# Partial sums reloaded into PSUM by ScalarE, head norms on VectorE, and maximum and exponential in one step, in a one-core hybrid mLSTM and attention block

## The chip, the cores and the metric

The kernel runs on one core of one Trainium2 chip. The metric is the device time of one execution, in microseconds; lower is better. Five engines run their own instruction queues in order: TensorE (PE), VectorE (DVE), ScalarE (ACT), GpSimd (POOL) and SyncE (SP), which here only issues DMAs.

## The reference

One transformer-like layer over 256 tokens of width 2048, all in float32:

```python
mod = jnp.einsum('bd,de->be', jax.nn.silu(c), w_ada[layer]) + b_ada[layer]
shift1, scale1, gate1, shift2, scale2, gate2 = jnp.split(mod[:, None, :], 6, axis=-1)
h = rms_norm(x, norm1_w[layer]) * (1 + scale1) + shift1
proj = h @ w_in[layer]
mq, mk, mv, mo, mi, mf, dq, dk, dv = jnp.split(proj, split_pts, axis=-1)
...
h_ml = mlstm_chunkwise(to_heads(mq, ML_DQK), to_heads(mk, ML_DQK), to_heads(mv, ML_DV), li, lf)
h_ml = rms_norm(jnp.transpose(h_ml, (0, 2, 1, 3)), mlstm_norm_w[layer])
...
dq = partial_rope(rms_norm(dq.reshape(B, S, DA_HEADS, 2, DA_DH), q_norm_w[layer]), positions)
dk = partial_rope(rms_norm(dk.reshape(B, S, DA_HEADS, 2, DA_DH), k_norm_w[layer]), positions)
o_da = diff_attention(dq, dk, dv, lam)
o_da = rms_norm(o_da, subln_w[layer]) * (1.0 - lambda_init)
mix = jnp.concatenate([h_ml, o_da], axis=-1) @ w_out[layer]
x = x + gate1 * mix
h = rms_norm(x, norm2_w[layer]) * (1 + scale2) + shift2
g, u = jnp.split(h @ w_gate_up[layer], 2, axis=-1)
x = x + gate2 * ((jax.nn.silu(g) * u) @ w_down[layer])
```

The six modulation vectors come from a matrix-vector product with 2048 x 12288 weights (w_ada). Attention has 8 heads with two softmax maps each; the mLSTM has 4 heads.

## The kernel before, in words

**Ticks.** All large products are cut into 392 ticks, called T0 to T391 below. One tick takes a half chunk of weights (128 x 1024), splits it into a high and a low part in float32r, and does 12 matmuls of 128x512: three products (high x high, low weight x high, high weight x low; lines 581 to 583) for two rows and two token blocks. Per tick ACT casts the high part `wh` (line 211, called at `weights_hi`), DVE subtracts for the low part `wl` (line 181, `weights_lo`), and SP loads the raw weights `r` (line 527; 3 buffers). `wh` and `wl` have 4 buffers each, so they can be made up to about three ticks ahead of the product that reads them.

**The order of the ticks.** T0 to T95 are the input projection, twelve column groups, in six sweeps over the 2048 rows (`SWEEPS`; row blocks p0 to p1 of 256 rows, where one tick is one block): T0-11 and T12-23 one block for each group, T24-43 two blocks for ten groups, T44-67 four blocks (4 to 8) for the six EARLY groups (attention q and k, mLSTM q and k), T68-79 six blocks (2 to 8) for the two attention v groups, T80-95 four blocks for the mLSTM v and output gates. T96-127 are the output projection (`wo`), T128-151, T152-187 and T188-223 three sweeps of the gate and up projection (`f0`, `f1`, `f2`), T224-303 its rest (`fr`), T304-391 the down projection (`dn`). The unit "one sweep over one group" is called a visit. A visit accumulates in one of two PSUM accumulators of 128x1024 (pool `psA`); when it ends, `project_done` puts the sum away in SBUF as `proj[g]`: the first visit of a group by an ACT copy, each later one by a DVE addition `proj + acc` (line 181).

**Small work between ticks.** Everything else is written as generators whose steps (separated by `yield`) the class `Plan` (lines 90 to 161) places between the half ticks: the modulation columns `modc` and the transposed, normalised activations `hh`/`hl` (`make_hT`), attention (`prep`, `attend`, `attend_values`, `finish_attention`), the mLSTM (`conv`, `ml_scores`, `ml_values`, `ml_norm`, `ml_out`) and the gate rows (`g1rd`, `g1rp`). `Plan` keeps an estimate `v` of how far DVE's queue is behind and `a` for ACT's; it issues no new step while either is above 2.3 us (VMAX, AMAX), and never two steps of one generator in one place. The steps use 4 further PSUM banks (`psM`). An engine that is not PE thus gets its instructions in the order in which `Plan` issues them, and PE's transposes and small matmuls stand between the ticks at places fixed at build time. What a tick needs (`ready`) is forced to be issued ahead of it by `plan.until`.

**Norms of the heads.** The reciprocal square roots of q, k (`prep`: `rsq`, `rsk` in scratch, results `sclq` and `rstk`), of the attention output (`finish_attention`: `of`) and of the mLSTM output (`ml_norm`: `mf`) start from an integer estimate on DVE (`rsqrt_first`, lines 190 and 192) and take three Newton steps of four instructions on POOL (`rsqrt_newton`, lines 401 to 404). The scaled maximum of a softmax map, `st`, is also a POOL multiplication (line 785).

**Modulation weights.** 192 tiles of 512 KB (`ada`, 4 buffers) come by DMA. 40 of them go to PE as matrix-vector products (`gv`, line 216), the others to DVE as a multiplication with an accumulated sum (line 185). `ADA_PLAN` and `due(i)` say how many must be used by which tick; `ada_idle` uses further ones where the estimated DVE queue is short. The last 32 (for gate2, `ada5`) are held back until the stage `fr`.

## Time and profile before

| | |
|---|---|
| runs, us | 1230.78, 1231.78, 1232.55; median 1231.78 |
| profiled execution | 1227.86 us, of it 1226.1 us from the first to the last instruction |
| mean granted TensorE clock | 0.992 |
| busy share of the span | PE 97%, DVE 69%, ACT 47%, POOL 4% |
| `wl` subtraction on DVE | 392 of 1221 ns |
| `wh` cast on ACT | 392 of 1058 ns |
| modulation tile on DVE | 152 of 1217 ns |

In a line of the timeline the first number is the start in us, the second the duration; the bracket gives the idle time of the engine ahead of the instruction, and the instruction that it waited for. Rows that follow each other without a bracket ran back to back; since DVE and ACT overlap the end of one instruction with the start of the next, the distance of two starts (1.14 us for two `wl`) is what an instruction costs there. For PE the distance of two 128x512 matmuls is 0.227 us at full clock, so that a tick takes 2.73 us.

### The profile page before, as it was taken

The numbers are of one execution on the slowest core, as the hardware profiler recorded it, in microseconds if no ns is written. First come the engines' busy times: TensorE is split into PE (matmuls) and PEld (weight loads), VectorE is DVE, ScalarE is ACT, GpSimd is POOL, SyncE is SP. The second block draws the span as 40 slices with busy tenths as digits, with TensorE's granted clock in tenths as the row PEclk, the third lists the DMA queues.
The fourth block names the chain that finished last, engine by engine and source line by source line (L and its number), as shares of the span: only waits on it lengthen the run. The fifth ranks groups of instructions, "written<-read, shape, count | busy, mean of one in ns | idle before, by whom it ended". The sixth has DMA issues, their size and how long they took to land.

```text
span 1226.1 us, 14849 instructions
## 1 busy us (share of the span) xinstructions
PE 1189.7 (97%) x5590; PEld 955.9 (78%) x5590; DVE 851.1 (69%) x1197; ACT 582.1 (47%) x791; POOL 50.4 (4%) x126
## 2 busy tenths in 40 slices
PE   6999899998999898999999999999999999999998
PEld 2767678777888686788888888888888878888886
DVE  3757968898888998879856667878555454545443
ACT  3754345565666345665444444444444443433342
POOL 1000001205022000000000000000000000000000
PEclk9999999999999999999999999999999999999999
DMA  9898987656578897899755547998655544646471
GB/s 343 320 363 321 376 324 251 252 207 234 183 257 314 315 355 279 307 337 344 276 186 184 188 169 291 353 351 319 233 178 196 189 172 172 225 169 238 157 257 52
DMA packets 63258, 313.81 MB, mean 256 GB/s; under 512 B 6993, under 2 KB 7377, under 8 KB 41169
## 3 DMA queue, kind: packets, MB, share of 16 engines
q1 hardware_dynamic: 63186, 312.86, 69.9%
q8 instruction: 44, 0.72, 0.2%
q14 instruction: 28, 0.23, 0.0%
HBM read 310.73 MB, written 2.10 MB: 255 GB/s over the span
## 4 chain that ended last, share of the span: by engine, by line
PE 77%; DVE 13%; issue 3%; DMA 2%; POOL 2%; ACT 2%; SPq 0%; DVEq 0%; POOLq 0%; ACTq 0%
DVE wl L181 5%; DVE ada L185 4%; DMA ada<-in_w_ada_dram 2%; PE acc('dn', 0)_7816 L583 2%; PE acc('dn', 0)_7816 L581 2%; PE acc('dn', 2)_8616 L583 2%; PE acc('dn', 2)_8616 L581 2%; PE acc('dn', 1)_8236 L583 2%; PE acc('dn', 1)_8236 L581 2%; PE acc('dn', 0)_7816 L582 2%; PE acc('dn', 2)_8616 L582 2%; PE acc('dn', 1)_8236 L582 2%; DVE proj L181 1%; PE gv L216 1%; PE at L220 1%
## 5 line engine op out<-in xcount | busy, mean ns | idle before, releaser
L181 DVE TENSOR_TENSOR wl<-r,wh 128x1024 fp32r<-128x1024 f32 x392 | 473.6, 1221 | 206.6 <-ACT wh L211 206.3
L211 ACT ACTIVATE wh<-r 128x1024 fp32r<-128x1024 f32 x392 | 410.5, 1058 | 391.3 <-DMA r<-in_w_gu_dram 42.1
L185 DVE SCALAR_TENSOR_TENSOR ada<-ada,silc 128x1024 f32<-128x1024 f32 x152 | 183.0, 1217 | 1.7 <-DMA ada<-in_w_ada_dram 1.7
L216 PE MATMUL gv<-ada,early 128*32 128x256 f32 x320 | 25.7, 424 | 11.9 <-DMA ada<-in_w_ada_dram 11.7
L581 PE MATMUL acc('dn', 0)_7816<-wh,aTh 128*128 128x512 f32 x88 | 35.9, 408 | 0.0
L583 PE MATMUL acc('dn', 0)_7816<-wh,aTl 128*128 128x512 f32 x88 | 34.3, 390 | 0.0
L582 PE MATMUL acc('dn', 0)_7816<-wl,aTh 128*128 128x512 f32 x88 | 34.3, 389 | 0.0
L581 PE MATMUL acc('dn', 1)_8236<-wh,aTh 128*128 128x512 f32 x88 | 34.2, 389 | 0.0
L582 PE MATMUL acc('dn', 1)_8236<-wl,aTh 128*128 128x512 f32 x88 | 34.2, 389 | 0.0
L583 PE MATMUL acc('dn', 1)_8236<-wh,aTl 128*128 128x512 f32 x88 | 34.2, 389 | 0.0
L581 PE MATMUL acc('dn', 2)_8616<-wh,aTh 128*128 128x512 f32 x88 | 34.2, 389 | 0.0
L582 PE MATMUL acc('dn', 2)_8616<-wl,aTh 128*128 128x512 f32 x88 | 34.2, 389 | 0.0
L583 PE MATMUL acc('dn', 2)_8616<-wh,aTl 128*128 128x512 f32 x88 | 34.2, 389 | 0.0
L216 PEld LDWEIGHTS gv<-ada,early 128*32 128x32 f32 x320 | 7.8, 113 | 27.3 <-DMA ada<-in_w_ada_dram 16.4
L211 ACT ACTIVATE hx<-pt,modc,gcol 128x256 f32<-128x256 f32 (+1 forms) x36 | 17.4, 535 | 17.7 <-PE pt L220 14.6
L181 DVE TENSOR_TENSOR hl<-hx,hh 128x512 fp32r<-128x512 f32 (+1 forms) x18 | 11.4, 631 | 18.8 <-ACT hh L211 18.7
L211 ACT ACTIVATE pm<-sc,st,sclq 128x256 f32<-128x256 f32 (+1 forms) x32 | 15.9, 513 | 12.0 <-POOL st L785 12.0
L211 ACT ACTIVATE aTh<-at 128x512 fp32r<-128x512 f32 x22 | 12.0, 596 | 20.0 <-PE at L220 20.0
L211 ACT ACTIVATE fp<-fp 128x1024 f32<-128x1024 f32 x6 | 6.4, 1062 | 29.4 <-DVE fp L181 29.4
L582 PEld LDWEIGHTS acc('dn', 0)_7816<-wl,aTh 128*128 128x128 f32 x88 | 16.5, 188 | 4.2 <-issue 1.0
L581 PEld LDWEIGHTS acc('dn', 0)_7816<-wh,aTh 128*128 128x128 f32 x88 | 16.5, 188 | 4.2 <-issue 1.0
L582 PEld LDWEIGHTS acc('dn', 2)_8616<-wl,aTh 128*128 128x128 f32 x88 | 16.5, 188 | 3.5
(958 smaller groups left out, 2985.9 us busy)
## 6 DMA issues: line engine op xcount, KB each, us to landing
ada<-in_w_ada_dram SPq DMA_DIRECT2D x192, 512.0 KB, 5.7
r<-in_w_gu_dram SPq DMA_DIRECT2D x76, 1024.0 KB, 6.3
r<-in_w_dn_dram SPq DMA_DIRECT2D x44, 1024.0 KB, 4.8
r<-in_w_in_dram SPq DMA_DIRECT2D x36, 1024.0 KB, 6.7
r<-in_w_out_dram SPq DMA_DIRECT2D x16, 1024.0 KB, 7.4
r<-in_w_in_dram SPq DMA_DIRECT2D x24, 512.0 KB, 5.9
r<-in_w_gu_dram SPq DMA_DIRECT2D x24, 512.0 KB, 4.3
x<-in_x_dram SPq DMA_DIRECT2D x4, 512.0 KB, 5.9
```

Source lines behind the costliest of these rows:

```text
L181: nc.vector.tensor_tensor(o, a, b, op=op)
L185: nc.vector.scalar_tensor_tensor(out=o, in0=a, scalar=s, in1=b, op0=op0, op1=op1, accum_out=accum)
L211: nc.scalar.activation(o, a, func, **kw)
L216: nc.tensor.matmul(o, l, r, start=start, stop=stop, **kw)
L220: nc.tensor.transpose(o, a, ident[:])
L581: nc.tensor.matmul(o, ah[:, s], wh[:, r], start=t["start"] and j == 0, stop=False)
L582: nc.tensor.matmul(o, ah[:, s], wl[:, r], start=False, stop=False)
L583: nc.tensor.matmul(o, al[:, s], wh[:, r], start=False, stop=t["stop"] and j == 1)
```

## The change

The order of the ticks' products stays as it is. Six things change around them.

1. **Partial sums go back into PSUM.** For the twelve visits of four or more row blocks (T44, 48, 52, 56, 60, 64, 68, 74, 80, 84, 88, 92) `load_acc` lets ACT copy `proj[g]` into the accumulator one tick ahead, the products add onto it, and at the end an ACT copy replaces the DVE addition.
2. **Newton steps on VectorE**, as nine instructions in place of twelve; the scaling of q and the scaled maximum `st` move from POOL to DVE too.
3. **One step fewer** in `attend` and `ml_scores`: the ACT exponentials are queued in the same step as DVE's maxima. `finish_attention` and `ml_norm` lose one `yield` each.
4. **The planner**: a step that may not be issued now is skipped (`continue`), not the end of the search, and works already begun may go on at a backlog of 4.8 us (VMORE).
5. **Modulation tiles** go to PE one by one as they arrive, not in pairs, and the last 32 are no longer held back; `ADA_PLAN` has new numbers.
6. **Start-up** interleaves four single tiles with the steps of the first normalisation.

```diff
+VMORE = 2.5
...
-            if not force and (self.v > VMAX or self.a > AMAX):
-                break
+            more = VMORE if w.last >= 0 else 0.0
+            if not force and (self.v > VMAX + more or self.a > AMAX + more):
+                continue
...
-    ada_limit = [len(items) - 32]
...
-    def ada_batch():
-        s, p, _ = items[ada_next[1]]
-        return 2 if on_pe(s, p) else 1
+    def ada_batch(limit, ready):
         s, p, q = items[ada_next[1]]
+        n = 0
+        while ada_next[1] + n < min(limit, ada_next[0]) and n < (4 - q if on_pe(s, p) else 1) and (
+                not ready or ada_ready[ada_next[1] + n] <= plan.t):
+            n += 1
+        return n
...
     def rsqrt_newton(y, b, x_):
         for _ in range(3):
-            nc.gpsimd.tensor_tensor(b, y, y, op=ALU.mult)
-            nc.gpsimd.tensor_tensor(b, b, x_, op=ALU.mult)
-            nc.gpsimd.tensor_scalar(b, b, -0.5, 1.5, op0=ALU.mult, op1=ALU.add)
-            nc.gpsimd.tensor_tensor(y, y, b, op=ALU.mult)
+            tt(b, y, y, ALU.mult)
+            stt(b, b, -0.5, x_, ALU.mult, ALU.mult)
+            stt(y, b, 1.5, y, ALU.add, ALU.mult)
...
+    def load_acc(i):
+        t = ticks[i] if i < len(ticks) else {"onto": None}
+        if t["onto"] is not None:
+            acc = accs[t["acc"]] = psA.tile([P, 1024], F32, name=f"acc{t['acc']}", tag="acc")
+            act(acc[:], t["onto"]()[:], AF.Copy)
+            loaded.add(t["acc"])
...
-        nc.tensor.matmul(o, ah[:, s], wh[:, r], start=t["start"] and j == 0, stop=False)
+        kw = dict(skip_group_check=True) if acc in loaded else {}
+        nc.tensor.matmul(o, ah[:, s], wh[:, r], start=t["start"] and j == 0 and not kw, stop=False, **kw)
...
             if p0 == 0:
                 proj[g] = slab(f"proj{g}")
+            if p0 == 0 or ("in", g, p0) in loaded:
                 act(proj[g][:], acc[:], AF.Copy)
             else:
                 tt(proj[g][:], proj[g][:], acc[:], ALU.add)
...
-            nc.gpsimd.tensor_scalar(dst, dst, 0.125, None, op0=ALU.mult)
+            ts(dst, dst, 0.125, None, ALU.mult)
...
-        nc.gpsimd.tensor_tensor(st[:, :, 2:4], st[:, :, 0:2], scale, op=ALU.mult)
-        yield 0
+        tt(st[:, :, 2:4], st[:, :, 0:2], scale, ALU.mult)
...
             red(mneg[:, h, t:t + 1], L[:, o:o + w + 1], ALU.max, negate=True)
-        yield 0
...
-            visit(("in", g, p0), True, True, lambda kb: hts[0][kb], w_in[g], f"in{g}", pairs(p0, p1), (), project_done(g, p0, p1))
+            visit(("in", g, p0), True, True, lambda kb: hts[0][kb], w_in[g], f"in{g}", pairs(p0, p1), (), project_done(g, p0, p1),
+                  (lambda g=g: proj[g]) if p1 - p0 >= 4 else None)
...
-        a, b = spans["fr"]
-        if i >= a + 4:
-            n = len(items) - 32 + 32 * (i - 3 - a) / (b - 24 - a)
...
-    for n in range(2):
+    for n in range(4):
         ada_dma(ada_use())
-        next(h0)
-    next(h0)
+        if n < 3:
+            next(h0)
...
+        load_acc(i + 1)
...
-ADA_PLAN = ((0, 12, 3), (1, 16, 4), (2, 28, 0), (3, 8, 0), (4, 4, 0), (5, 4, 0), ("wo", 16, 22), ("f0", 24, 5), ("f1", 32, 5), ("f2", 8, 8))
+ADA_PLAN = ((0, 12, 3), (1, 16, 3), (2, 26, 2), (3, 12, 0), (4, 8, 0), (5, 14, 0), ("wo", 16, 22), ("f0", 24, 5), ("f1", 32, 5), ("f2", 24, 8))
```

The lines of the helpers move down by two (the addition from 181 to 183, the multiplication with a sum from 185 to 187, ACT's from 211 to 213, PE's small matmuls from 216 to 218 and its transposes from 220 to 222); the three products are on lines 593 to 595.

**Order on DVE, the first attention norm** (between T78 and T80; `of` is the scratch of the norm, `o` the attention output that waits for it, `proj_518` the k projection of heads 4 to 7, numbers behind a name count tiles). Before, after the integer estimate the Newton steps run on POOL, and DVE goes on to other work:

```order
L185 SCALAR_TENSOR_TENSOR of_269<-rs_0_148 128x8
L185 SCALAR_TENSOR_TENSOR of_269<-osq_150,of_269 128x8
L190 TENSOR_SCALAR of_269<-of_269 128x8
L192 TENSOR_SCALAR of_269<-of_269 128x8
L181 TENSOR_TENSOR proj_518<-proj_518,rstk 128x512 x2
L181 TENSOR_TENSOR rpk<-proj_518,rope_kc 128x128 x2
L181 TENSOR_TENSOR rpk<-proj_518,rope_ks 128x128 x2
L181 TENSOR_TENSOR proj_518<-rpk 128x16x8 x2
L181 TENSOR_TENSOR wl_2674<-r_2447,wh_2659 128x1024
L181 TENSOR_TENSOR o_2539<-o_2539,of_269 128x1024
```

After, the nine steps follow at once, and the multiplication of `o` stands behind them:

```order
L187 SCALAR_TENSOR_TENSOR of_269<-rs_0_148 128x8
L187 SCALAR_TENSOR_TENSOR of_269<-osq_150,of_269 128x8
L192 TENSOR_SCALAR of_269<-of_269 128x8
L194 TENSOR_SCALAR of_269<-of_269 128x8
L183 TENSOR_TENSOR of_269<-of_269 128x8
L187 SCALAR_TENSOR_TENSOR of_269<-of_269 128x8 x2
L183 TENSOR_TENSOR of_269<-of_269 128x8
L187 SCALAR_TENSOR_TENSOR of_269<-of_269 128x8 x2
L183 TENSOR_TENSOR of_269<-of_269 128x8
L187 SCALAR_TENSOR_TENSOR of_269<-of_269 128x8 x2
L183 TENSOR_TENSOR o_2702<-o_2702,of_269 128x1024
L183 TENSOR_TENSOR wl_2809<-r_2608,wh_2798 128x1024
```

No instruction of another engine stands between the estimate and `o` any more.

**Order on DVE, ahead of the low parts of T72 and T73** (names as numbered tiles). Before, one modulation tile and a third of the mLSTM's convolution stand there:

```order
L181 TENSOR_TENSOR wl71_2390<-r70_2237,wh71_2382 128x1024
L185 SCALAR_TENSOR_TENSOR ada2_3_0_2131,gsum_100<-ada2_3_0_2131,silc0_124 128x1024
L181 TENSOR_TENSOR wl72_2415<-r72_2293,wh72_2398 128x1024
L185 SCALAR_TENSOR_TENSOR cv1_2311<-cvt11_2302,part_75,cv1_2311 128x255 x2
L185 SCALAR_TENSOR_TENSOR cv1_2311<-cvt11_2302,part_75,cv1_2311 128x254 x2
L185 SCALAR_TENSOR_TENSOR cv1_2311<-cvt11_2302,part_75,cv1_2311 128x253 x2
L181 TENSOR_TENSOR wl73_2437<-r72_2293,wh73_2429 128x1024
```

After, `wl72` stands behind the whole k norm of heads 4 to 7 (its end is shown: two of the three Newton steps, then a modulation tile):

```order
L187 SCALAR_TENSOR_TENSOR rstk_147<-rsk1_2435,rstk_147 128x2x8
L183 TENSOR_TENSOR rsk1_2435<-rstk_147 128x2x8
L187 SCALAR_TENSOR_TENSOR rsk1_2435<-rsk1_2435 128x2x8
L187 SCALAR_TENSOR_TENSOR rstk_147<-rsk1_2435,rstk_147 128x2x8
L183 TENSOR_TENSOR rsk1_2435<-rstk_147 128x2x8
L187 SCALAR_TENSOR_TENSOR rsk1_2435<-rsk1_2435 128x2x8
L187 SCALAR_TENSOR_TENSOR rstk_147<-rsk1_2435,rstk_147 128x2x8
L187 SCALAR_TENSOR_TENSOR ada2_2_3_2012,gsum_100<-ada2_2_3_2012,silc1_125 128x1024
L183 TENSOR_TENSOR wl72_2530<-r72_2329,wh72_2517 128x1024
L183 TENSOR_TENSOR proj3_521<-proj3_521,rstk_147 128x512 x2
L183 TENSOR_TENSOR wl73_2548<-r72_2329,wh73_2538 128x1024
```

This norm stood six low parts later before, behind `wl77`.

## The prediction on record

> **What bounds the kernel now.** I read the page's busy shares first, then the busy time by stretches of the span, then PE's timeline for every bracket (an idle time and its releaser), then what the releasing engine did before.
>
> ```profile
> span 1226.1 us, 14849 instructions
> PE 1189.7 (97%) x5590; PEld 955.9 (78%) x5590; DVE 851.1 (69%) x1197; ACT 582.1 (47%) x791; POOL 50.4 (4%) x126
> ```
>
> PE is the bound and has 36 us of idle time. The stretches say where (us, then busy time of PE, PEld, DVE, ACT, POOL, the granted clock, DMA share, GB/s):
>
> ```profile
> 137.00:171.00 34.00, 27.36 (x150) 19.45 (x148) 25.07 (x37) 9.56 (x13) 0.00 (x0) 0.95 0.92 347
> 187.00:379.00 192.00, 185.03 (x940) 151.16 (x939) 167.17 (x325) 116.12 (x248) 41.30 (x94) 0.99 0.65 231
> 379.00:436.00 57.00, 53.43 (x229) 41.92 (x228) 53.35 (x93) 29.33 (x43) 5.79 (x12) 0.97 0.88 325
> 515.00:1215.00 700.00, 700.00 (x3132) 578.11 (x3130) 436.38 (x464) 304.30 (x318) 0.00 (x0) 1.00 0.64 232
> ```
>
> From 515 to 1215 us PE never idles: nothing can be won there, only lost. The change can win in 137 to 436 us (T30 to T111), and there DVE is no spare engine: 87% busy in the second row, 94% in the third. The idle times of PE, with their releasers, are few:
>
> ```profile
> 142.89 0.64 PE L216 MATMUL gv<-ada,early 128*32 128x256 f32 x8 [1.91 <-DMA ada<-in_w_ada_dram]
> 144.16 0.64 PE L216 MATMUL gv<-ada,early 128*32 128x256 f32 x8 [0.63 <-DMA ada<-in_w_ada_dram]
> 150.15 0.64 PE L216 MATMUL gv<-ada,early 128*32 128x256 f32 x8 [1.83 <-DMA ada<-in_w_ada_dram]
> 162.37 0.64 PE L216 MATMUL gv<-ada,early 128*32 128x256 f32 x8 [0.48 <-DMA ada<-in_w_ada_dram]
> 164.79 0.64 PE L216 MATMUL gv<-ada,early 128*32 128x256 f32 x8 [1.78 <-DMA ada<-in_w_ada_dram]
> ...
> 227.44 1.09 PE L220 MATMUL tpk<-ident,proj 128*128 128x128 f32 x8 [1.29 <-DVE proj L181]
> 240.95 0.74 PE L220 MATMUL aT<-ident,pm 128*128 128x128 f32 x3 [0.30 <-ACT wh L211]
> 250.84 0.27 PE L216 MATMUL sc<-bmask,identb 128*128 128x256 bf16 x1 [0.50 <-ACT pm L211]
> 257.82 0.55 PE L220 MATMUL aT<-ident,pm 128*128 128x128 f32 x3 [0.71 <-ACT pm L211]
> ...
> 306.90 1.97 PE L220 MATMUL ot<-ident,o 128*128 128x128 f32 x8 [4.15 <-DVE o L181]
> 308.66 1.55 PE L220 MATMUL tpk<-ident,proj 128*128 128x128 f32 x8
> ...
> 418.90 2.02 PE L216 MATMUL g1rp<-g1rd,ones 128*128 128x512 f32 x2 [3.52 <-DVE g1rd L181]
> 419.93 1.42 PE L581 MATMUL acc('wo', 0)_3396<-wh,mlh 128*128 128x512 f32 x1
> 421.14 0.63 PE L582 MATMUL acc('wo', 0)_3396<-wl,mlh 128*128 128x512 f32 x1
> 421.57 0.63 PE L583 MATMUL acc('wo', 0)_3396<-wh,mll 128*128 128x512 f32 x1
> 422.00 0.56 PE L581 MATMUL acc('wo', 0)_3396<-wh,mlh 128*128 128x512 f32 x1
> 422.39 0.39 PE L582 MATMUL acc('wo', 0)_3396<-wl,mlh 128*128 128x512 f32 x1
> ```
>
> Three clusters: modulation tiles that arrive late (6.6 us), attention (2.8 and 4.15 us), the gate rows (3.52 us). The waits cost more than their length, since a slow clock follows. Eight transposes take 1.09 us at 227.44, but 1.97 and 1.55 behind the wait of 4.15: 1.3 us more. Behind 3.52 the products' starts are 1.21, 0.43, 0.43 and 0.39 us apart, not 0.227: with the slow pair ahead of them some 2 us. It can follow short waits too, as in T38:
>
> ```profile
> 167.27 0.63 PE L581 MATMUL acc('in', 9, 2)_1444<-wh,hh 128*128 128x512 f32 x1
> 168.55 0.63 PE L581 MATMUL acc('in', 9, 2)_1444<-wh,hh 128*128 128x512 f32 x1
> ```
>
> Three products in 1.28 us are 0.427 each; eleven of them lose 2.2 us, and the last waits ahead were 0.48 and 1.78. The Trainium skill ("TensorE: Matmul & The Clock Gate", Part 1: The HAM clock gate) says that the clock halves only after an idle window of about 3.4 us. By that rule the new waits of 1 to 3 us below would cost only their length; by T38 any cluster of them may cost 2.2 us on top. The measurement decides, and I carry the 2.2 into the upper end, not the sum.
>
> **The change part by part.** Times are against the profiled execution, 1227.86 us (span 1226.1), which is 3.9 us below the median of the runs.
>
> *Newton and scaling on DVE.* A small DVE instruction and the POOL chain:
>
> ```profile
> 219.65 0.17 DVE L192 TENSOR_SCALAR rsk<-rsk 128x16 f32<-128x16 f32 x1
> 219.85 0.17 DVE L190 TENSOR_SCALAR rsk<-rsk 128x16 int32<-128x16 int32 x1
> 220.06 0.18 DVE L192 TENSOR_SCALAR rstk<-rsk 128x16 int32<-128x16 int32 x1
> ...
> 297.86 0.17 DVE L192 TENSOR_SCALAR of<-of 128x8 int32<-128x8 int32 x1
> ...
> 305.39 0.20 POOL L404 TENSOR_TENSOR of<-of 128x8 f32<-128x8 f32 x1
> 305.62 1.22 DVE L181 TENSOR_TENSOR o<-o,of 128x1024 f32<-128x1024 f32 x1 [1.51 <-POOL of L404]
> ```
>
> Starts lie 0.2 us apart. Eight norms of 9, two scalings and eight `st` are 82 instructions, 16.4 us onto DVE. In exchange `o` follows its estimate after 9 x 0.2 = 1.8 us, where POOL took from 297.86 to 305.6 (it was busy with the k norm until 300.3). The wait of 4.15 and its 1.3 of slow clock go: minus 5.5.
>
> POOL's operations also stretch beside DVE's:
>
> ```profile
> 302.90 1.21 DVE L181 TENSOR_TENSOR wl<-r,wh 128x1024 fp32r<-128x1024 f32 x1
> ...
> 302.92 1.26 POOL L403 TENSOR_SCALAR of<-of 128x8 f32<-128x8 f32 x1
> ```
>
> The POOL step took 1.26 us, the other 0.20, for as long as `wl` ran; `wl` kept its 1.21. The Trainium skill ("SBUF", on the port pair that VectorE and GpSimd share) says that whoever comes first holds it and the other blocks. By the rule DVE would also win back time when POOL falls silent; by these rows only POOL paid, so I book nothing.
>
> *Partial sums into PSUM.* The group rows and one copy and one addition:
>
> ```profile
> L181 DVE TENSOR_TENSOR wl<-r,wh 128x1024 fp32r<-128x1024 f32 x392 | 473.6, 1221 | 206.6 <-ACT wh L211 206.3
> L185 DVE SCALAR_TENSOR_TENSOR ada<-ada,silc 128x1024 f32<-128x1024 f32 x152 | 183.0, 1217 | 1.7 <-DMA ada<-in_w_ada_dram 1.7
> 33.62 1.03 ACT L211 ACTIVATE proj<-acc('in', 0, 0)_302 128x1024 f32<-128x1024 f32 x1 [1.12 <-PE acc('in', 0, 0)_302 L583]
> 200.35 1.22 DVE L181 TENSOR_TENSOR proj<-proj,acc('in', 0, 4)_1621 128x1024 f32<-128x1024 f32 x1 [2.36 <-PE acc('in', 0, 4)_1621 L583]
> ```
>
> Twelve additions at 1.14 us (the distance of starts) leave DVE: minus 13.7. ACT gets 24 copies of about 1.03, 24.7 us, on its 116 of 192. A copy into PSUM has no row here; its bounds are 1.03 and, if that direction were as slow as the `o` row, 1.22. Each load is queued a tick (2.73) ahead of its product, ahead of one `wh`, so it is hidden; uncovered it would cost about 1 us a visit. PE gains nothing by itself. With the additions gone and Newton added, DVE is 2.7 us worse off, and some modulation tiles come earlier. By counting the rows of the order and these prices, DVE has 225 us of work for `wl44` to `wl111` before and 227 after.
>
> *Steps closer together* (one step for maximum and exponential, the planner). DVE's sum is the same, but its lumps are larger. Worst is what stands between `wl69` and `wl74`: the q1 norm (reduction 1.21, 13 small 2.6, rotary 1.5), four mLSTM maxima 1.25, mLSTM scores and decays 2.1, the k1 norm (1.21 and 12 small, 3.6), k's product and rotary 2.8, three tiles 3.5, five `wl` 5.7: 24.3 us, against 15.8 before. PE needs 5 x 2.73 = 13.65 and some 2.5 of small matmuls. With all four `wl` buffers full DVE is ahead by 2.6 ticks, 7.1, and PE waits 1; with one tick ahead it waits 5.4. I take 2.5, since DVE was 87% busy there and seldom far ahead. The same sum for T93 to T107 gives 0 to 5; I take 3. The last attention heads (T85 to T93) and `ot` of the second group follow their DVE steps more closely: 0 to 4, I take 2.
>
> *The first q.*
>
> ```profile
> 204.30 1.04 ACT L211 ACTIVATE sqq<-proj 128x1024 f32<-128x1024 f32 x1
> ...
> 206.42 1.21 DVE L196 TENSOR_REDUCE rsq<-sqq 128x16 f32<-128x1024 f32 x1
> ```
>
> Its transposes now stand 2.5 ticks (6.8 us) behind T47, not 3.5. The chain: copy 1.03, square 1.04, reduction 1.2, 13 small 2.6, rotary 1.5, with one or two `wl` between, 8.5 to 9.7. A wait of 2 to 3 replaces the 2.8 of the attention cluster: zero in the sum.
>
> *Tiles to PE one by one.* The tile of 142.89 is wanted ahead of T32, a tick sooner; it arrives when it did, so its wait grows to about 4.6, with no gain. But the later ones (1.83, 0.48, 1.78) now stand a tick further back and vanish, with T38's 2.2: minus 6.3, plus 2.1, plus up to 2 of slow clock behind a wait of 4.6, as behind 4.15. Minus 2.5.
>
> *Gate rows.* Modulation comes earlier, and the four `g1rp` are spread over T94 to T101 and not forced: minus 3.52 and 2.0 of clock, minus 5.5.
>
> *Held-back tiles.* Of 32 tiles some 23 fall into T188 to T223 (98 us), which lies in this stretch:
>
> ```profile
> 645.00:760.00 115.00, 115.00 (x531) 94.87 (x530) 76.96 (x71) 54.09 (x60) 0.00 (x0) 1.00 0.57 194
> ```
>
> DVE has 77 of 115, so 66 of 98, and gets 23 x 1.22 = 28: 94, or 96%. Transfers rise by 11.5 MB, 117 GB/s, to 311, under the 347 shown above. Each `wl` may be three ticks early, which covers it: zero, and if that cover fails 1.14 us for each tile too many. Start-up: one tile's wait is moved, 0 to 1.7; I take 0.5.
>
> Sum: 0.5 - 2.5 + 0 + 2.5 - 5.5 + 2 - 5.5 + 3 = -5.5 us: 1222.4 for an execution like the profiled one, 1226.3 at the median.
>
> **The rivals.**
>
> - *DVE takes PE's place in T66 to T107 (slower).* For: 24.3 us of work against 16.2 of PE, a 94% row. Then the bundled steps cost their full 5.4, 5 and 4, q another 1, two clusters the clock's 2.2; tiles win nothing: 0.5 + 0 + 1 + 5.4 + 2.2 - 5.5 + 4 - 5.5 + 5 + 2.2 = +9.3, about 1241. It decides where DVE reaches `wl70` less than one tick ahead. Against: six of DVE's additions leave in T44 to T68, just ahead. Chance 0.26.
> - *The waits go and none come (larger gain).* DVE enters each lump with four buffers full: -5.5, -5.5, -4.2 for the tiles, -2.8: -18 at most, about -13 with a few small waits: 1219. For: 13.7 us less of additions. Against: the lump of 24.3. Chance 0.16.
> - *Nothing changes.* The waits move to other places but DVE's sum for T44 to T111, 225 against 227, sets when that stretch ends: within 2.5 us. Chance 0.17.
> - *The held-back tiles fill DVE or the queues in T188 to T223,* where `wl` and a tile take 1.14 + 1.14 of 2.73 us and weights compete: some four tiles too many: +4 on the forecast, 1230. Chance 0.08, spread over the three outcomes.
>
> **How the numbers follow.** The forecast, a gain of 2.5 to 10 us, has 0.33. 2.5 us is 0.2%, about what a measurement of this kernel can tell from no change. Faster: 0.33 + 0.16 + 0.02 = 0.51; same 0.17 + 0.03 = 0.20; slower 0.26 + 0.03 = 0.29. The range: from 1215 (the large gain, with more than its mean) to 1242 (the slow case); beyond lie the full sums, 1213.8 and about 1249. The forecast's own range is 1221.8 to 1229.3.
>
> **What would show it.** Right: no wait before `ot` of the first group nor at `g1rp`; PE released by DVE `wl` near T71 to T74 by 2 to 3 us; one wait of 4 to 5 before T32, none at 150 and 165; DVE additions 12 fewer; PE still full beyond 515 us. Wrong: waits on `wl` above 5 us between T70 and T107 (DVE bound), brackets in T188 to T223, accumulator loads that release a product, or a wait that stays at `ot` although its norm is short.

## The result and the profile after

The changed kernel takes 1246.78 us (median of four runs, 1246.70 to 1248.73), the kernel before 1232.16 beside it (1230.78 to 1233.56): a ratio of 1.0122, 95% interval 1.0105 to 1.014. It is 14.6 us slower. The profiled execution of after is the slowest of its four (1248.73) and that of before (1227.86) faster than all of its four, so the two traces lie 20.9 us apart; stretches are compared within them, and the medians carry the verdicts.

The first lines of the page of after:

```profile
span 1247.0 us, 14848 instructions
PE 1197.8 (96%) x5590; PEld 957.4 (77%) x5590; DVE 854.5 (69%) x1267; ACT 603.5 (48%) x817; POOL 3.3 (0%) x20
```

POOL is nearly empty and DVE has 3.4 us more, as the change says. PE's busy time grew by 8.1 us with the same 5590 instructions, which is clock (0.992 granted on average before, 0.987 after), and its idle time by 12.8.

First products of the same tick, before and after, show where the spans part: T44 at 186.87 and 189.83, T74 at 286.15 and 315.43, T96 at 379.06 and 406.38, T128 at 482.38 and 503.19, T224 at 755.42 and 776.28. So after loses 3.0 us up to T44, 26.3 in T44 to T73, then gains 8.5 up to T128. The two stretches of before (first fence) and three of after (us, busy time of PE, PEld, DVE, ACT, POOL, granted clock, DMA share, GB/s):

```profile
187.00:286.00 99.00, 96.19 (x473) 77.26 (x472) 89.81 (x167) 59.63 (x103) 16.05 (x35) 1.00 0.68 240
286.00:435.00 149.00, 141.27 (x692) 114.98 (x691) 129.78 (x246) 85.14 (x187) 31.04 (x72) 0.98 0.72 260
```

```profile
190.00:318.00 128.00, 110.50 (x523) 88.36 (x523) 102.59 (x240) 82.54 (x141) 0.00 (x0) 0.95 0.53 188
318.00:457.00 139.00, 132.19 (x641) 106.30 (x641) 121.89 (x253) 83.95 (x175) 0.00 (x0) 1.00 0.79 291
535.00:1235.00 700.00, 698.75 (x3123) 576.68 (x3122) 438.61 (x465) 301.67 (x317) 0.00 (x0) 1.00 0.64 232
```

In the stretch that loses, PE is idle for 17.5 us and its clock is 0.95; DVE is busy 80%, ACT 64%. No engine is full there: they wait for each other. PE's waits in after, and the first `ot` of after, which has none:

```profile
147.60 1.08 PE L218 MATMUL gv<-ada,early 128*32 128x256 f32 x8 [5.21 <-DMA ada<-in_w_ada_dram]
200.36 0.50 PE L593 MATMUL acc('in', 0, 4)_1594<-wh,hh 128*128 128x512 f32 x1 [1.77 <-ACT hh L213]
218.14 1.25 PE L222 MATMUL tpq<-ident,proj 128*128 128x128 f32 x8 [3.83 <-DVE proj L183]
237.87 1.09 PE L222 MATMUL tpk<-ident,proj 128*128 128x128 f32 x8 [2.04 <-DVE proj L183]
247.84 1.10 PE L222 MATMUL cvt<-ident,proj 128*128 128x128 f32 x8 [0.90 <-ACT pm L213]
267.35 1.97 PE L222 MATMUL cvt<-ident,proj 128*128 128x128 f32 x8 [2.94 <-ACT pm L213]
287.13 0.67 PE L218 MATMUL L<-ml,upper 128*128 128x257 f32 x2 [1.72 <-DVE ml L187]
297.96 1.97 PE L222 MATMUL tpq<-ident,proj 128*128 128x128 f32 x8 [4.31 <-ACT ml L213]
...
336.08 1.04 PE L222 MATMUL ot<-ident,o 128*128 128x128 f32 x8
...
394.85 1.06 PE L222 MATMUL ot<-ident,o 128*128 128x128 f32 x8 [2.42 <-DVE o L183]
401.31 1.13 PE L218 MATMUL g1rp<-g1rd,ones 128*128 128x512 f32 x2 [0.40 <-DVE odl L187]
433.91 0.50 PE L594 MATMUL acc('wo', 0)_3459<-wl,mlh 128*128 128x512 f32 x1 [1.81 <-DVE wl L183]
...
686.67 0.50 PE L594 MATMUL acc('gu', 1, 5)_5608<-wl,hh 128*128 128x512 f32 x1 [0.76 <-DVE wl L183]
```

Seven waits, 17.5 us, lie in T44 to T73, where before had 2.8. None is a late `wl`: one is a product that waits for its activations `hh` (1.77), the others are small matmuls waiting for a chain of small steps on DVE and ACT, or for a bank (`tpq` and `cvt` do not read `ml` or `pm`; they write into a bank that those exponentials still read). Behind 2.94 and 4.31 eight transposes take 1.97 us; behind 2.04 they take 1.09. Ahead of the 4.31 ACT itself stood idle for DVE's maxima and then loaded a function table:

```profile
295.88 1.28 ACT L213 ACT_TABLE_LOAD   x1 [5.38 <-DVE mneg L198]
```

Such loads take 1.28 us each. After has 13 of them, before 11 (7 and 5 from T44 to T111); what the two more cost PE was not separated.

### The profile page after: what moved, and what is told of

Read it like the earlier page. It is cut to its first block, busy times and chain, and to the rows that moved or that the text cites. A ratio compares the mean times of both kernels' runs of the same rounds, so it can differ in the third digit from the quotient of the medians.

```text
span 1247.0 us, 14848 instructions
## 1 busy us (share of the span) xinstructions
PE 1197.8 (96%) x5590; PEld 957.4 (77%) x5590; DVE 854.5 (69%) x1267; ACT 603.5 (48%) x817; POOL 3.3 (0%) x20
## 4 chain that ended last, share of the span: by engine, by line
PE 71%; DVE 15%; DMA 5%; ACT 4%; issue 4%; SPq 0%; DVEq 0%; ACTq 0%
DVE wl L183 5%; DVE ada L187 4%; DMA ada<-in_w_ada_dram 3%; DMA r<-in_w_gu_dram 2%; PE acc('dn', 0)_7804 L595 2%; PE acc('dn', 0)_7804 L594 2%; PE acc('dn', 2)_8604 L594 2%; PE acc('dn', 1)_8224 L595 2%; PE acc('dn', 1)_8224 L594 2%; PE acc('dn', 2)_8604 L595 2%; PE acc('dn', 2)_8604 L593 2%; PE acc('dn', 0)_7804 L593 2%; PE acc('dn', 1)_8224 L593 2%; PE gv L218 2%; ACT wh L213 1%
## 5 line engine op out<-in xcount | busy, mean ns | idle before, releaser
L593 PE MATMUL acc('dn', 0)_7804<-wh,aTh 128*128 128x512 f32 x88 | 35.9, 408 | 0.0
L595 PE MATMUL acc('dn', 0)_7804<-wh,aTl 128*128 128x512 f32 x88 | 34.3, 390 | 0.0
L594 PE MATMUL acc('dn', 0)_7804<-wl,aTh 128*128 128x512 f32 x88 | 34.3, 389 | 0.0
L593 PE MATMUL acc('dn', 1)_8224<-wh,aTh 128*128 128x512 f32 x88 | 34.2, 389 | 0.0
L594 PE MATMUL acc('dn', 1)_8224<-wl,aTh 128*128 128x512 f32 x88 | 34.2, 389 | 0.0
L595 PE MATMUL acc('dn', 1)_8224<-wh,aTl 128*128 128x512 f32 x88 | 34.2, 389 | 0.0
L593 PE MATMUL acc('dn', 2)_8604<-wh,aTh 128*128 128x512 f32 x88 | 34.2, 389 | 0.0
L594 PE MATMUL acc('dn', 2)_8604<-wl,aTh 128*128 128x512 f32 x88 | 34.2, 389 | 0.0
L595 PE MATMUL acc('dn', 2)_8604<-wh,aTl 128*128 128x512 f32 x88 | 34.2, 389 | 0.0
L593 PEld LDWEIGHTS acc('dn', 0)_7804<-wh,aTh 128*128 128x128 f32 x88 | 16.5, 188 | 4.3 <-issue 1.0
```

The source lines that it names most:

```text
L593: nc.tensor.matmul(o, ah[:, s], wh[:, r], start=t["start"] and j == 0 and not kw, stop=False, **kw)
L594: nc.tensor.matmul(o, ah[:, s], wl[:, r], start=False, stop=False, **kw)
L595: nc.tensor.matmul(o, al[:, s], wh[:, r], start=False, stop=t["stop"] and j == 1, **kw)
```

## Experiments: one part undone

Theories: **A**, the small matmuls stand nearer in PE's queue than their chains take, through the planner; **B**, the Newton steps overload DVE; **C**, ACT's accumulator copies hold the casts behind them; **D**, the modulation tiles; later **E**, the merged step returns banks too soon, and **F**, its exponentials hold the casts on ACT. Ratios are against the kernel before on the same chip.

**u_plan**

```diff
-            more = VMORE if w.last >= 0 else 0.0
-            if not force and (self.v > VMAX + more or self.a > AMAX + more):
-                continue
+            if not force and (self.v > VMAX or self.a > AMAX):
+                break
```

> The changed kernel with the planner's old rule (one limit of 2.3 us for all works, and the search ends at the first step that may not be issued). Theory A (dependent matmuls now stand nearer in PE's queue than their chain on DVE and ACT takes): most of the 14.6 us come back, 1232 to 1238, and the waits before tpq, tpk, cvt and L between T44 and T74 (17.5 us in all) fall below 9. Theory B (Newton steps and scalings overload DVE): it stays within 3 us of 1246.8. Theory C (ACT's copies of accumulators stand at the head of its queue and hold the casts behind them): within 3 us of 1246.8. Theory D (modulation tiles): within 3 us of 1246.8.

1247.02 us, ratio 1.0131 (1.0106 to 1.0156), in the interval of the other theories. A's number missed: in its trace the waits that A named fall to 3.0 us and T44 to T73 loses 12.8 us, not 26.3, but others come there (`sc` 3.69, `aT` 2.80), and waits of 2.7 to 3.4 us further on take the gain back.

**u_newton**

```diff
-            tt(b, y, y, ALU.mult)
-            stt(b, b, -0.5, x_, ALU.mult, ALU.mult)
-            stt(y, b, 1.5, y, ALU.add, ALU.mult)
+            nc.gpsimd.tensor_tensor(b, y, y, op=ALU.mult)
+            nc.gpsimd.tensor_tensor(b, b, x_, op=ALU.mult)
+            nc.gpsimd.tensor_scalar(b, b, -0.5, 1.5, op0=ALU.mult, op1=ALU.add)
+            nc.gpsimd.tensor_tensor(y, y, b, op=ALU.mult)
```

> The changed kernel with the Newton steps and q's scaling back on POOL (twelve instructions each); the planner then books less for DVE and places a few steps one to four ticks sooner still. Theory A: no gain, within 4 us of 1246.8 or slower, since the chains get longer and the matmuls stand as near. Theory B: 1236 or less. Theories C and D: within 3 us of 1246.8.

1254.47 us, 1.0188 (1.0162 to 1.0213). Slower still: B falls as the cause.

**u_load**

```diff
-                  (lambda g=g: proj[g]) if p1 - p0 >= 4 else None)
+                  None)
```

> The changed kernel without the reloading of PSUM: the twelve additions are on DVE again, and the planner, which books them, places most small steps 3 to 12 ticks later, with many forced at T96 and T98. Theory A: the waits between T44 and T74 fall by half, but forced steps at T96 to T98 wait 10 us or more: 1240 to 1256. Theory B: DVE is loaded more, 1250 or more. Theory C: the waits before tpq fall and the sum gains 5 us or more, 1242 or less. Theory D: within 3 us of 1246.8.

1255.39 us, 1.0194 (1.017 to 1.0219), in A's interval and in B's. In its trace the kernel is 5 us ahead of before at T96, and 31 behind at T100: the planner, which books the additions, has put off the last heads until they are forced. The run therefore tells nothing on B or C.

**u_ada**

```diff
+    ada_limit = [len(items) - 32]
...
+        return 2 if on_pe(s, p) else 1
...
-            if q + n == 4:
+            if q == 2:
...
-ADA_PLAN = ((0, 12, 3), (1, 16, 3), (2, 26, 2), (3, 12, 0), (4, 8, 0), (5, 14, 0), ("wo", 16, 22), ("f0", 24, 5), ("f1", 32, 5), ("f2", 24, 8))
+ADA_PLAN = ((0, 12, 3), (1, 16, 4), (2, 28, 0), (3, 8, 0), (4, 4, 0), (5, 4, 0), ("wo", 16, 22), ("f0", 24, 5), ("f1", 32, 5), ("f2", 8, 8))
```

> The changed kernel with the old handling of modulation tiles (pairs to PE, the last 32 held back until the last part of the gate and up projection, old numbers) and the old start-up. Theory D (the tiles cost it): 1236 or less. Theory A: the start-up's 3 to 5 us come back and the last hT pair stands one tick earlier, but the waits before the transposes stay: 1241 to 1246. Theories B and C: as A.

1245.98 us, 1.0112 (1.0079 to 1.0145), in A's interval. D's number missed. T24 starts 0.9 us behind before and not 4.8, so the start-up's loss is real, but it is not what decides the sum.

**gap** (q's and k's transposes later, and banks returned half a tick later)

```diff
             rope_products(nm, t)
+        yield 0
+        yield 0
         yield 2
...
-        plan.rel(2)
         yield 0
+        plan.rel(2)
```

> The changed kernel with only places moved: q's and k's transposes two half ticks later, and the PSUM banks of the scores counted as free half a tick after their exponentials are queued, not with them (so cvt and tpq stand later). Theory A (PE's small matmuls stand nearer than their chains take): the waits before tpq, tpk and cvt, 14 us of 17.5 between T44 and T74, fall below 5 and the slow clock behind them goes: 1234 or less. Theory B (DVE's load) and theory D (modulation tiles): no gain, 1244 or more, since the work is the same and DVE gets no relief.

1254.99 us, 1.0188 (1.0165 to 1.021). A's sum missed, and B and D had this number; but the waits that A named fell to 3.0 us (`tpq` 1.11, `cvt` 1.88), as it said. The same `tpq` in u_plan, in gap and in u_newton:

```profile
216.25 1.09 PE L220 MATMUL tpq<-ident,proj 128*128 128x128 f32 x8 [2.46 <-DVE proj L181]
```

```profile
215.39 1.09 PE L222 MATMUL tpq<-ident,proj 128*128 128x128 f32 x8 [1.11 <-DVE proj L183]
```

```profile
214.47 1.09 PE L222 MATMUL tpq<-ident,proj 128*128 128x128 f32 x8 [1.80 <-DVE proj L183]
```

In after it stands 2.5 ticks behind T47's end and waits 3.83. In u_plan it stands half a tick further back: 3.83 - 1.36 = 2.47. In gap a whole tick: 3.83 - 2.73 = 1.10. In u_newton it has the same place, but the ten Newton steps and scaling are not on DVE ahead of the rotary products. The first and the last of these ten and the first rotary product, in the timeline of after:

```profile
214.69 0.18 DVE L183 TENSOR_TENSOR rsq<-sclq 128x16 f32<-128x16 f32 x1
...
216.58 0.17 DVE L192 TENSOR_SCALAR sclq<-sclq 128x16 f32<-128x16 f32 x1
216.66 0.48 DVE L183 TENSOR_TENSOR rpq<-proj,rope_qc 128x128 f32<-128x128 f32 x2
```

They take 216.66 - 214.69 = 1.97, which leaves 1.86, and 1.80 was measured. This wait is place against chain, to 0.06 us. But gap's heads then meet other chains (`aT` 4.45, `L` 2.56): from T68 to T73 it loses 15.6 us.

**u_step**

```diff
         tt(st[:, :, 2:4], st[:, :, 0:2], scale, ALU.mult)
+        yield 0
...
             red(mneg[:, h, t:t + 1], L[:, o:o + w + 1], ALU.max, negate=True)
+        yield 0
```

> The changed kernel with the maximum and the exponential in two steps again (and the removed empty steps back), the scaled maximum still on DVE. Theory E (the merged step gives banks back half a tick sooner, and PE meets the exponential that still reads them): the waits released by an exponential (ACT pm 0.9 and 2.94, ACT ml 4.31, ACT pm 1.21) go, the waits before tpq0 and tpk0 (3.83 and 2.04, DVE) stay: 1236 to 1242. Theory A with the planner as its cause: within 4 us of 1246.8.

1263.54 us, 1.0257 (1.0236 to 1.0277), missed by both. No part, undone, brings the time back: every undoing also re-sorts the small work.

## Experiments: one part alone

**o_plan**

```diff
+            more = VMORE if w.last >= 0 else 0.0
-            if not force and (self.v > VMAX or self.a > AMAX):
-                break
+            if not force and (self.v > VMAX + more or self.a > AMAX + more):
+                continue
```

> The kernel before with only the planner's new rule (skip instead of stop, 4.8 us for works already begun). Theory A with the planner as its cause: 1240 to 1248, waits of PE at small matmuls in T44 to T96 of 15 us and more (10.5 before). Theory E or the sum of several parts: 1228 to 1237.

1231.27 us, 1.0002 (0.999 to 1.0015). The planner's rule alone costs nothing, and u_plan without it gained nothing. A with the planner alone as the cause falls; places against chains, as at `tpq`, do not fall with it.

**o_step**

```diff
-        nc.gpsimd.tensor_tensor(st[:, :, 2:4], st[:, :, 0:2], scale, op=ALU.mult)
-        yield 0
+        tt(st[:, :, 2:4], st[:, :, 0:2], scale, ALU.mult)
...
             red(mneg[:, h, t:t + 1], L[:, o:o + w + 1], ALU.max, negate=True)
-        yield 0
```

> The kernel before with only the merged steps (maximum, scaled maximum on DVE, exponential; two empty steps gone). Theory E: slower, 1234 to 1240, with new waits of PE on ACT's exponentials. Theory A with the planner as its cause: within 3 us of before, since without the looser rule the steps don't crowd.

1243.75 us, 1.0093 (1.007 to 1.0116): more than E gave, with waits of 5.4 us at `aT` and 5.6 at `po` that are not bank waits.

**b_v25**

```diff
-VMAX = AMAX = 2.3
+VMAX = AMAX = 2.5
```

> The kernel before with one constant of the planner changed (limit 2.5 us, not 2.3): no operation changes, only places, mostly by half a tick to three ticks sooner. Theory A, in its strong form (any new arrangement loses, the old one is a fortunate one): 1236 or more. If only the crowding of the merged steps costs: within 4 us of before.

1228.37 us, 0.998 (0.9965 to 0.9995). A new arrangement need not lose; the strong form of A falls.

**o_ada** (parts 5 and 6 of the change on the kernel before)

```diff
-    ada_limit = [len(items) - 32]
...
-            if q == 2:
+            if q + n == 4:
...
-            ada_dma(ada_use())
+            n = ada_batch(due(i), False)
+            if n == 0:
+                break
+            ada_dma(ada_use(n))
```

> The kernel before with only the new handling of the modulation tiles (one by one to PE, none held back, new numbers, new start-up). Theory D: 1240 or more. If the start-up costs its 1 to 3 us and the wait before T32 what it did in the changed kernel, with gains at the gate rows: 1229 to 1238.

1256.65 us, 1.0213 (1.0194 to 1.0231), in D's interval. But up to T96 it is 11.5 us ahead of before, at T100 26 behind: four ticks take 51 us, since the heads that the tiles had put off are forced there. The changed kernel has no such stretch (T96 to T99 take 13.6 us), and u_ada won nothing, so D is not its cause.

## Experiments: PE's order held

The h runs add a part to the kernel before with the planner's bookings left as they were, so that all PE instructions stand in their old order. Now only the operations' own cost shows.

**h_of** and **h_newton**

```diff
+    def newton_dve(y, b, x_):
+        for _ in range(3):
+            nc.vector.tensor_tensor(b, y, y, op=ALU.mult)
+            nc.vector.scalar_tensor_tensor(out=b, in0=b, scalar=-0.5, in1=x_, op0=ALU.mult, op1=ALU.mult)
+            nc.vector.scalar_tensor_tensor(out=y, in0=b, scalar=1.5, in1=y, op0=ALU.add, op1=ALU.mult)
...
-        rsqrt_newton(f, b, xx)
+        newton_dve(f, b, xx)
```

> The kernel before with one edit: only the two attention-output norms take their Newton steps on DVE, and the planner books nothing for them, so that every instruction of PE keeps its place. Theory A (the new places of the small matmuls cost, not the operations): the wait of 4.15 before ot and the slow clock behind it go, 4 to 6 us faster, 1225 to 1227. Theory B (Newton loads DVE): same or slower.

1228.25 us, 0.9981 (0.9967 to 0.9995): 2 us, half of what was expected. The wait at `ot` fell from 4.15 only to 2.54, as in this order `o` stands behind the k product, its rotary steps and a `wl` (302.39 to 306.08); the k product's own wait for POOL is 0.52.

> The kernel before with all eight norms, q's scaling and the scaled maxima on DVE, booked at nothing, so that every PE instruction keeps its place. Theory A: 1224 to 1231, since waits on POOL go (4.15 at ot) and at most 2 us come before tpq. Theory B: 1238 or more, with waits on wl.

h_newton puts `newton_dve` in all three places and the scalings on DVE as well: 1233.69 us, 1.0024 (1.0011 to 1.0038). 3.4 us slower: 2.7 above A's interval and 4.3 below B's. The wait at the first `ot` is 3.76 here.

**h_load** and **h_load_after**

```diff
-            act(acc[:], t["onto"]()[:], AF.Copy)
+            nc.scalar.activation(acc[:], t["onto"]()[:], AF.Copy)
...
+            elif ("in", g, p0) in loaded:
+                nc.scalar.activation(proj[g][:], acc[:], AF.Copy)
+                plan.v += 1024 / 960 + 0.07
```

> The kernel before with only the partial sums reloaded into PSUM, the planner still booking the additions on DVE, so that every PE instruction keeps its place. Theory A: within 3 us of before. Theory C (ACT's copies hold the casts behind them): 1236 or more, with casts and products late at the ends of visits.

1238.90 us, 1.0073 (1.0055 to 1.0091): C holds. One end of a visit in its timeline, ACT, DVE and PE (before has 0.71 at this `aT`):

```profile
256.97 1.03 ACT L700 ACTIVATE proj<-acc('in', 1, 4)_2064 128x1024 f32<-128x1024 f32 x1 [1.38 <-PE acc('in', 1, 4)_2064 L595]
257.89 1.05 ACT L211 ACTIVATE wh<-r 128x1024 fp32r<-128x1024 f32 x1
258.98 1.23 DVE L181 TENSOR_TENSOR wl<-r,wh 128x1024 fp32r<-128x1024 f32 x1 [1.97 <-ACT wh L211]
260.53 0.55 PE L220 MATMUL aT<-ident,pm 128*128 128x128 f32 x3 [2.23 <-ACT pm L211]
```

The copy waits at ACT's head for the last product; the cast and the exponentials `pm` stand behind it, and DVE and PE wait for these. The first such copy in after, in T48, waits 6.79 us, and the `wl` behind it stands ahead of the q chain that `tpq` waits for:

```profile
207.10 1.03 ACT L213 ACTIVATE proj<-acc('in', 0, 4)_1594 128x1024 f32<-128x1024 f32 x1 [6.79 <-PE acc('in', 0, 4)_1594 L595]
209.11 1.22 DVE L183 TENSOR_TENSOR wl<-r,wh 128x1024 fp32r<-128x1024 f32 x1 [2.96 <-ACT wh L213]
```

h_load_after moves one thing, the copy out of a reloaded accumulator behind the next cast:

```diff
+        late = i > 0 and ticks[i - 1]["acc"] in loaded and pending
-        for fn in pending:
-            fn()
-        pending = []
+        if not late:
+            for fn in pending:
+                fn()
+            pending = []
         load_acc(i + 1)
...
         weights_hi(i + AHEAD)
+        for fn in pending:
+            fn()
+        pending = []
```

> The kernel before with the partial sums reloaded, as in the run of 1238.9 us, but ACT's copy out of the accumulator queued behind the next cast of weights, not ahead of it. Theory C (the copy waits at the head of ACT's queue for the end of the visit and holds the cast): 5 us or more come back, 1234 or less. If ACT's 25 us more of work cost by themselves: 1237 or more.

1231.81 us, 1.0003 (0.999 to 1.0015). All of it comes back: not ACT's 25 us of work cost, but the copy at the head of its queue.

**h_step** (exponentials in the step of the maxima; bookings and banks as before)

```diff
-        nc.gpsimd.tensor_tensor(st[:, :, 2:4], st[:, :, 0:2], scale, op=ALU.mult)
-        yield 0
+        nc.vector.tensor_tensor(st[:, :, 2:4], st[:, :, 0:2], scale, op=ALU.mult)
+        was = plan.a
...
+        cost, plan.a = plan.a - was, was
+        yield 0
+        plan.a += cost
```

> The kernel before with the exponentials queued on ACT in the same step as DVE's maxima (scaled maximum on DVE), bookings and the banks' release as before, every PE instruction in its old place; casts of weights now stand behind exponentials that wait for the maxima. Theory F (ACT's head waits for DVE and holds the casts): 1236 to 1243, as the merged step with new places took 1243.8. If only its places cost: 1228 to 1233.

1245.32 us, 1.0118 (1.0101 to 1.0136), 2.3 us above F's interval and 12 above the other: F's mechanism holds and is dearer than forecast, and E isn't needed, as banks are returned when they were. ACT loads 11 function tables here, as before. The chain in its timeline, ACT, DVE and PE:

```profile
238.74 1.28 ACT L211 ACT_TABLE_LOAD   x1 [7.50 <-DVE st L785]
...
243.95 2.96 ACT L211 ACTIVATE wh<-r 128x1024 fp32r<-128x1024 f32 x3
245.06 1.23 DVE L181 TENSOR_TENSOR wl<-r,wh 128x1024 fp32r<-128x1024 f32 x1 [5.16 <-ACT wh L211]
246.66 0.75 DVE L185 SCALAR_TENSOR_TENSOR pm<-pm,st 128x128 f32<-128x128 f32 x2
247.16 0.99 PE L220 MATMUL aT<-ident,pm 128*128 128x128 f32 x3 [5.62 <-DVE pm L185]
```

and before at the same place:

```profile
237.87 0.57 ACT L211 ACTIVATE pm<-sc,st,sclq 128x256 f32<-128x256 f32 x1 [4.12 <-POOL st L785]
239.84 1.06 ACT L211 ACTIVATE wh<-r 128x1024 fp32r<-128x1024 f32 x1
```

ACT stood idle for 7.50 us at its head, waiting for DVE's maxima; two heads' exponentials followed; three casts were late; DVE then waited 5.16 for a cast with the `pm` products behind its `wl`; PE waited 5.62 for them. Before, ACT's wait had a cast ahead of it and one between the two heads. The totals of that wait of DVE between 187 and 400 us (total, times, longest; before has no such row), in h_load, h_load_after, h_step, after and a_held:

```profile
DVE wl L181 <- ACT wh L211: 24.4, 12, 4.2
```

```profile
DVE wl L181 <- ACT wh L211: 8.2, 5, 2.8
```

```profile
DVE wl L181 <- ACT wh L211: 15.5, 8, 5.2
```

```profile
DVE wl L183 <- ACT wh L213: 13.7, 9, 3.0
```

```profile
DVE wl L187 <- ACT wh L217: 6.1, 5, 2.3
```

**h_ops** (the edits of h_load and h_newton together)

```diff
-            act(acc[:], t["onto"]()[:], AF.Copy)
+            nc.scalar.activation(acc[:], t["onto"]()[:], AF.Copy)
...
-        rsqrt_newton(dst, b, xx)
+        newton_dve(dst, b, xx)
```

> The kernel before with both exchanges of engines (partial sums reloaded by ACT; all norms, scalings and scaled maxima on DVE), the planner booking as before, every PE instruction in its old place. If the two costs add (8.6 and 3.4 us alone): 1241 to 1244, so the operations alone explain most of the change's 15 us. If they share one slack (additions off DVE make room for the Newton steps): 1234 to 1238, and the places explain the larger part.

1239.01 us, 1.0071 (1.0049 to 1.0093), between the two forecasts. The costs, 8.6 and 3.4, do not quite add.

**a_held** is the changed kernel with PE's order held and two moves on ACT: the copy behind the cast as in h_load_after, and the exponentials queued half a tick later.

```diff
     def run(self, force=False, only=None):
+        for fn in self.later:
+            fn()
+        self.later = []
...
-            act(pm[t, m], o, AF.Exp, bias=st[:, t, 2 + m:3 + m], scale=scale[:, t, m:m + 1],
+            defer(pm[t, m], o, AF.Exp, bias=st[:, t, 2 + m:3 + m], scale=scale[:, t, m:m + 1],
```

> The changed kernel with every PE instruction in its place and only two moves on ACT: the copy out of a reloaded accumulator behind the next cast of weights, and the exponentials queued half a tick later, so that where a new tick begins the cast stands ahead of them. Theories C and F (ACT's head waits and holds the casts, and DVE then waits for ACT): 6 us or more come back, 1241 or less. Theory A (the places on PE): within 4 us of 1246.8.

1243.77 us, 1.0098 (1.008 to 1.0115), some 3 us below the change and in A's interval. C and F expected 6 and more, so for the changed kernel they explain a part only. DVE's waits for casts are 6.1 us here, less than the 8.2 of h_load_after, which costs nothing; so most of the 11.6 us by which a_held is still slower than before seems to come from elsewhere. In its trace `tpq` waits 1.33 (3.83) and `tpk` 0.65 (2.04), and T44 to T73 loses 19 us, not 26. The bank waits, 2.96 at `cvt` and 4.31 at `tpq`, stay as they were: this order on ACT does not set them. That places do is argued, not shown.

**best** (b_v25 with h_of's edit)

```diff
-VMAX = AMAX = 2.3
+VMAX = AMAX = 2.5
...
-        rsqrt_newton(f, b, xx)
+        newton_dve(f, b, xx)
```

> The kernel before with the two edits that were faster alone: the planner's limit at 2.5 us (0.998) and the attention-output norms on DVE, booked at nothing (0.998). If they add: 1225 to 1227. If both only move the same wait before ot: 1228 to 1230.

1230.52 us, 0.9994 (0.9979 to 1.001), just above both forecasts. The two small gains do not add; no version beats the kernel before by more than the 0.2% of each alone.

## Why the prediction was wrong, point by point

It forecast 1226.3 us and measured 1246.8, above its range. By the first products of the ticks, the two traces part in two places. Up to T24 after loses 4.8 us, where the prediction had 0.5 for the start-up. In T44 to T73 it loses 26.3, where the prediction had 2.5 for steps closer together and zero for the first q and for the partial sums. The rest came near the forecast: after gains 1.8 from T30 to T43 (2.5 forecast), 2.0 from T74 to T95 (5.5 - 2), 5.5 from T96 to T111 (5.5 - 3).

So the step that failed is the price of T44 to T73. It counted delay there as late `wl`, out of DVE's sum of work. None of the seven waits that came is for a `wl`: they are for chains that pass through ACT and DVE in turn, or for a bank. The steps one by one:

- *"PE gains nothing by itself" and each load "is hidden"* (partial sums into PSUM). The copies out were counted as 12 of ACT's 24 copies, but not as waits: each waits at ACT's head for the end of its visit, with the next cast behind it. Plus 8.6 in h_load, all of it back in h_load_after. The prediction had named what is queued behind a waiting instruction on DVE and PE, and not on ACT. This is the first failure.
- *"DVE's sum is the same, but its lumps are larger"* (steps closer together). The second failure: the merged step was costed on DVE alone. ACT's exponentials now wait for DVE at the head of a queue that holds the casts, and DVE waits for those casts: plus 14 in h_step. No rival had that loop.
- *The lump before `wl74`, 2.5, as waits on `wl`.* No such wait came. The waits there, 1.72 and 4.31, are of `L` for DVE's decays and of `tpq` for a bank.
- *The first q, zero in the sum.* The third failure: the chain was put at 8.5 to 9.7 us; from the end of T47 (206.90) to the transposes it took 11.2, as two casts, a tile and two `wl` lay between: 3.83, then 2.04 at `tpk`.
- *"The waits go" at the first `ot`, minus 5.5.* Right: in after it has no wait and its transposes take 1.04 us, not 1.97. It took the new order as well as the short norm, since in the old places 2.54 is left (h_of).
- *The last heads and the `ot` of the second group, plus 2.* Somewhat under-sized: that `ot` now waits 2.42, and an `sc` 1.21.
- *Gate rows, minus 5.5.* Right: 0.40 is left of 3.52, and T96 to T111 take 50.6 us after 56.1.
- *Tiles, minus 2.5.* Right: one wait of 5.21 (4.6 forecast), none later; from T30 to T44 after makes up 1.8 us. But the start-up costs 4.8 up to T24, and 0.9 with the old start-up and tiles (u_ada); what it waits for was not traced.
- *T93 to T107, plus 3.* Right in size: `wl` waits of 1.81, 0.38 and 0.40.
- *Held-back tiles, zero.* Nearly: PE waits 0.76 and 0.35 on `wl`, and loses 1.9 us from T188 to T223.
- *Clock.* Cited from the Trainium skill ("TensorE: Matmul & The Clock Gate", Part 1: The HAM clock gate) was an idle window of about 3.4 us. Here the clock fell behind shorter waits too, as behind 2.94 (eight transposes in 1.97), but not behind every one (1.09 behind 2.04); the measurement decides. PE's busy time grew by 8.1 us, more than the 2.2 that the upper end carried for each of two clusters.
- *The rival "DVE takes PE's place"* had the right sign and the wrong mechanism: DVE is busy 80% in the stretch that loses (102.59 of 128.00 us), 91% in the same stretch before (89.81 of 99.00). The "about 1249" at the upper end has no sum shown for it.

What stays open: the parts' own costs with held places (8.6, 3.4, 14) are more than the change's 14.6 (the second and the third both hold the scaled maxima on DVE), and undoing any one part gives no gain, since each re-sorts the rest. That ACT's order costs is shown for the parts alone. In the changed kernel a_held shows 3 of the 14.6 us for it; the rest was not separated into places, bank waits, table loads and start-up.

## What to carry to other kernels

Ask of every instruction that is moved to another engine what it waits for there and what is queued behind it: a copy or an exponential that waits at the head of the queue which also feeds the bound engine's operands can cost more than its own length, however idle that engine is. When two engines wait for each other in turn, a share of busy time tells little; look for the rows in which each is the other's releaser. To price an edit in a program whose order a planner decides, hold the order first and change only the operation; undoing parts one by one measured mostly the re-sorting here.

## What the runs showed of the hardware

The length of one wait of PE did not tell whether a slow clock follows. Eight transposes took 1.97 us behind an idle time of 2.94 us in after, but 1.10 behind 2.96 at the same place in a_held; behind 2.04 they took 1.09 in after and 1.65 in u_step. Behind 1.77 us in after the small `gt` matmuls start 0.21 us apart, in before 0.12; the granted clock is 0.72 there (200 to 206 us). A copy of 128x1024 from SBUF into PSUM on ACT, which no row of before showed, took 1.01 to 1.06 us, as long as the way back (1.03); the first in the timeline of after:

```profile
185.84 1.03 ACT L213 ACTIVATE acc('in', 0, 4)_1594<-proj 128x1024 f32<-128x1024 f32 x1 [2.51 <-DVE proj L183]
```
